# Second products' pools restacked, context steps spread, modulation stepped in the input projection

## Chip, cores, metric

The kernel runs on one core of a Trainium2 chip. The time is that of one launch on the device, in microseconds (us); runs are given by their median.

The engines are TensorE (PE, matrix products), VectorE (DVE), ScalarE (ACT) and GpSimd (POOL); SyncE (SP) issues most transfers between the chip's main memory and the on-chip memory. Each engine takes its instructions in order.

## What is computed

One trunk layer, for one group of 128 context tokens and one of 1024 latent tokens that share their weights, with D = 1024, 8 query and 2 key heads of 128, and an FFN of width 2816:

```python
def _swiglu(h, w1, w2):
    a, b = jnp.split(h @ w1, 2, axis=-1)
    return (jax.nn.silu(a) * b) @ w2
...
    sh1, sc1, g1, sh2, sc2, g2, sh3, sc3, g3 = [mod[:, i][:, None, :] for i in range(N_MOD)]
    f1 = _swiglu(_modulate(x, sh1, sc1), lw['ffn1_w1'], lw['ffn1_w2'])
    x = _layer_norm(ALPHA * x + 0.5 * g1 * f1, lw['ln_g'][0], lw['ln_b'][0])
    mix, k, v = _mixer(_modulate(x, sh2, sc2), lw, rope, kv_ctx)
    x = _layer_norm(ALPHA * x + g2 * mix, lw['ln_g'][1], lw['ln_b'][1])
    f2 = _swiglu(_modulate(x, sh3, sc3), lw['ffn2_w1'], lw['ffn2_w2'])
    x = _layer_norm(ALPHA * x + 0.5 * g3 * f2, lw['ln_g'][2], lw['ln_b'][2])
```

`_mixer` projects its input to queries, keys, values, pooling inputs (`pin`) and two gates, runs attention and a pooling branch side by side, and merges them. The modulation vectors are `silu(cond) @ w_mod + b_mod`, once for the context and once for the latents. All is float32.

## The kernel before

**Arithmetic.** Every float32 operand is split into a high and a low part: ACT writes the high part (L109), DVE subtracts it for the low one (L110). A product is then three matmuls (L132 to L134): high by high, high by low, low by high. `weight` loads a weight tile into one of five places `raw`, shared by all stages, and splits it into two `op` tiles. Splits of the second products' left operand are `so`, from a loaded tile `sr`.

**Stages**, in time: first FFN, up products (to 570 us) and second products (to 789); input projection of the mixer (to 1200); attention and pooling (to 1510); output side of the mixer (to 1761); second FFN, up products (to 2306) and second products (to the end). The projection works on three groups of 384 tokens (`project`, g = 0, 1, 2); attention begins while the last `pin` blocks are still to be done.

**The FFN.** Both products are formed by a scheme of seven products in place of eight (the up products A11, A12, S1, S2, S4, S3, A22; the second ones M1 to M7). `up` runs 18 pairs of column blocks (`up_pair`, m = 4 to 21). The second operand of A22 is the last to be read. In a pair, S3 and A22 add into the same PSUM bank Y; between them DVE has to read Y (`s5 += Y`, L572), and after A22 ACT takes its silu (L576).

**Work beside.** `tick` steps the generators in `side`: in the up stages the FFN of the context tokens (155 steps), in the projection the key and query tiles (norm, rotation, transposes on PE). When `side` is empty, a tick steps `mods` instead, the modulation of a later stage: a load of 512 KB of `w_mod` into a `raw` place and two DVE instructions with accumulation (L192, output `junk`), one to a step. `up_prod` ticks once or twice per product and steps `mods` once after A12, S2 and A22. In the projection `feature_block` (one weight tile, 24 matmuls of 384 columns) ticks once, `group_down` (the query weights, eight chunks of 18 matmuls) once per chunk. What is left of `mods` at the end of the projection is run in one go:

```python
                xT = nxt
            for _ in self.mods:
                pass
            self.flush()
```

**Memory.** At the end of the up stage its pools close, and `open_pools` opens the down stage's pools in the order of the list it is given, stacked from the lowest free address up. A tile of a down pool must wait until the up tiles that lay in its place have been read. In bytes per partition the stack before is, for the first FFN: `so` at 101920 to 126496, `op` to 151072, `sr` to 163360, then the rest. The first `so` lies over the place of the up stage's `op` tile that holds the weights of the last A22; places 126496 and up belonged to operands read earlier. For the second FFN it is: `op` at 92704 to 141856, `rest` to 162468, `so` to 211680, `sr` to 228064; the first `so` tiles lie over operands (`b2`) that the last A22 reads.

A scheduler then orders the instructions of each engine by a simulated time, so code order is not the order on an engine.

Of the kernel before, what the change touches and what calls it, by code (L numbers as in the profile page):

```python
# [32 lines left out]
P = 128  # L33
D = 1024
# [20 lines left out]
class Layer:  # L55
# [20 lines left out]
    def tick(self, n=1):  # L76
        for _ in range(n):
            while self.side:
                try:
                    next(self.side[0])  # L80
                    break
                except StopIteration:
                    self.side.popleft()
            else:
                next(self.mods, None)

    def flush(self):
        while self.side:
# [442 lines left out]
    def up_pair(self, m, w1, h_d):  # L531

        nc = self.nc
        add, sub = (partial(nc.vector.tensor_tensor, op=o) for o in (ALU.add, ALU.subtract))
        halves = lambda t: (t[:, :512], t[:, 512:])
        ra, rb = self.raw(w1[2 * m]), self.raw(w1[2 * m + 1])
        (b11, b21), (b12, b22) = halves(ra), halves(rb)
        hi, lo = self.wide(ra)
        Y = self.bank()
        self.up_prod(Y, "A11", (hi[:, :512], lo[:, :512]), True)  # L540
        s1 = self.tmp()
        nc.scalar.activation(s1, Y, AF.Copy)
        yield
        t = self.tsum()
        sub(t[:, 0, :], b12, b11)
        sub(t[:, 1, :], b22, t[:, 0, :])
        t12 = self.wide(self.flat(t))
        Z = self.bank()
        self.up_prod(Z, "A12", (hi[:, 512:], lo[:, 512:]), True, 2)
        add(s1, Z, s1)  # L550
        nc.scalar.activation(s1, s1, AF.Silu)
        yield
        w22 = self.wide(b22, 512)
        X = self.bank()
        self.up_prod(X, "S1", [halves(w)[0] for w in t12], True)
        s5 = self.tmp()
        nc.scalar.activation(s5, X, AF.Copy)
        yield
        sub(b11, t[:, 1, :], b11)
        sub(b21, b21, t[:, 1, :])  # L560
        t34 = self.wide(ra)
        self.up_prod(Y, "S2", [halves(w)[1] for w in t12], False, 2)
        u2 = self.tmp()
        nc.scalar.activation(u2, Y, AF.Copy)
        yield
        self.up_prod(X, "S4", w22, False)
        add(u2, X, u2)
        nc.vector.tensor_tensor(u2, u2, s1, ALU.mult)
        self.keep_h(m, 0, u2, h_d)
        yield  # L570
        self.up_prod(Y, "S3", [halves(w)[0] for w in t34], False)
        add(s5, Y, s5)  # L572
        yield
        self.up_prod(Y, "A22", [halves(w)[1] for w in t34], False)
        sa = self.tmp()
        nc.scalar.activation(sa, Y, AF.Silu)  # L576
        nc.vector.tensor_tensor(s5, s5, sa, ALU.mult)  # L577
        self.keep_h(m, 1, s5, h_d)
        self.h_sums(m, u2, s5, h_d)
        yield  # L580
# [200 lines left out]
        self.flush()  # L781

    def ctx_sum(self, i):
        y = self.t([P, 2, 512], "yc", bufs=1)
        with self.tc.issue_after(self.last_load):
            self.nc.sync.dma_start(self.flat(y), self.fc_d[i])
        return y

    def norms(self, i, res_of, dst):
# [8 lines left out]
        def residual(t):  # L798
            if last_stage(i):
                res = self.t([P, D], "tc", bufs=6, pool=self.pools["tc"])  # L800
            else:
                res = self.t([P, D], "res", bufs=2)
            with self.tc.issue_after(self.last_load):
                nc.sync.dma_start(res, res_of(t))
            return res

        def last(t, y):

            tt, stt = nc.vector.tensor_tensor, nc.vector.scalar_tensor_tensor
            res = residual(t)  # L810
            rs, mu, m2 = (self.t([P, 1], n) for n in ("rs", "mu", "mu2"))
            halves = [(y[:, h, :], slice(h * 512, (h + 1) * 512)) for h in range(2)]
            (y0, c0), (y1, c1) = halves
            for (v, cs), out in zip(halves, (None, m2)):
# [19 lines left out]
        def norm(t, y):  # L834
            y = self.flat(y)
            gate = gc if t == 0 else gl
            res = residual(t)
            rs = self.t([P, 1], "rs")
            mu = self.t([P, 1], "mu")
            nc.vector.tensor_tensor(y, y, gate, ALU.mult)  # L840
            yield
            nc.vector.scalar_tensor_tensor(y, res, ALPHA, y, ALU.mult, ALU.add, accum_out=mu)
# [13 lines left out]
    def ffn(self, i, head, res_of, dst, order, half, beside=None):  # L856
        a, tc = self.a, self.tc
        s = str(1 + i // 2)
# [15 lines left out]
        if beside:  # L874
            beside()
        with ExitStack() as st:
            self.open_pools(st, "down" + s, ("tc", "xr", "y", "so", "op", "sr", "rest") if i == 0 else ("tc", "y", "op", "rest", "so", "sr"))
            self.op_bufs = 6 if i == 0 else 12
            self.ph = self.pools["rest"]
            self.down(i // 2, a["w2_" + s], h_d, lambda: self.norms(i, res_of, dst), order, half, last_stage(i))  # L880
# [51 lines left out]
    def group_down(self, units, lhs):  # L932
        acc = [[self.bank() for _ in range(3)] for _ in range(2)]
        n = units.shape[0]
        for kc in range(n):
            w = self.weight(units[kc])
            self.tick()
            for j in range(3):
                self.down_unit(acc, w, lhs[kc], j, kc == 0, kc == n - 1)
        return acc  # L940
# [125 lines left out]
    def feature_block(self, w, xT):  # L1066
        wh, wl = self.weight(w)
        acc = self.bank()
        for kc in range(KC):
            if kc == 2:  # L1070
                self.tick()
            ks = slice(kc * P, (kc + 1) * P)
            x = xT[kc]
            self.mm3(acc[:, :GT], (wh[:, ks], wl[:, ks]), (x[:, 0, :], x[:, 1, :]), kc == 0, kc == KC - 1)
# [448 lines left out]
```

## Time and profile before

| | us |
|---|---|
| median of 3 runs | 2543.17 |
| range of the runs | 2539.73 to 2545.66 |
| profiled execution, its own time | 2543.56 |
| its span in the trace | 2541.8 |
| PE busy | 2459.1 |
| DVE busy | 1830.0 |
| ACT busy | 1213.7 |

The share of PE's busy time says how much standing still there is in all. The waits of PE say where it is and which instruction ended each wait; an instruction named `w` is a PSUM bank, `b` an up operand, `x` an input of the projection. The windows give the granted clock of TensorE in a stretch as a share of full speed: 1.00 is 2.4 GHz, 0.50 is 1.2 GHz, and a number between says how much of the stretch was at each. The timeline gives the start of each instruction, its duration, and in brackets the idle time before it and what ended it.

### The profile page before, as it was taken

What the parts mean: (1) busy time and instruction counts of PE and PEld (TensorE: products, weight loads), DVE (VectorE), ACT (ScalarE), POOL (GpSimd) and SP (SyncE); (2) the same over time, 40 slices, a digit from 0 to 9 for tenths busy, and PEclk for the clock granted to TensorE, in tenths of its full rate; (3) what the DMA queues carried; (4) which work ended last, traced back from release to release, by engine and by line L of the source; (5) the groups of instructions that cost most, each with busy time, mean ns of one, the idle gap of its engine ahead of it and who ended that gap; (6) DMA issues with size and microseconds to landing.
All of it is one profiled execution on the core that took longest, in us unless ns stands there. A gap on an engine that the chain in (4) does not pass through costs nothing.

```text
span 2541.8 us, 34077 instructions
## 1 busy us (share of the span) xinstructions
PE 2459.1 (97%) x12232; PEld 2121.8 (83%) x12232; DVE 1830.0 (72%) x2806; ACT 1213.7 (48%) x2092; POOL 462.4 (18%) x683
## 2 busy tenths in 40 slices
PE   8999999989999999999899999998899999998998
PEld 4888888868788989989899999997688888886886
DVE  6777778867678656468878876765777666766777
ACT  5544444434445344443777773433644444434442
POOL 0000011110023212132467640110000001011002
PEclk9999999999999999999999999999999999999999
DMA  7455567668675645545200024564455546568673
GB/s 290 137 180 184 183 233 246 225 228 290 215 257 209 221 173 176 177 142 187 79 2 1 1 97 159 205 213 151 137 192 179 178 165 229 195 220 305 233 249 124
DMA packets 163185, 461.63 MB, mean 182 GB/s; under 512 B 18756, under 2 KB 33396, under 8 KB 163016
## 3 DMA queue, kind: packets, MB, share of 16 engines
q1 hardware_dynamic: 140472, 377.60, 44.4%
q0 software_dynamic: 22400, 81.60, 8.6%
q8 instruction: 96, 1.57, 0.3%
q14 instruction: 73, 0.60, 0.1%
q10 hardware_dynamic: 144, 0.26, 0.0%
HBM read 388.32 MB, written 71.07 MB: 181 GB/s over the span
## 4 chain that ended last, share of the span: by engine, by line
PE 77%; issue 10%; DVE 5%; DMA 4%; ACT 2%; POOL 2%; SPq 0%; POOLq 0%; DVEq 0%; ACTq 0%
PE w L132 22%; PE w L134 22%; PE w L133 22%; PE w L928 8%; PE w L137 3%; DMA raw<-w 1%; DVE op L110 1%; DMA raw<-x 1%; DVE mx L1238 1%; DVE x L110 1%; DVE junk L192 1%; DMA raw<-w_mod 1%; PE w L226 0%; DMA sr<-h 0%; ACT pr L1246 0%
## 5 line engine op out<-in xcount | busy, mean ns | idle before, releaser
L110 DVE TENSOR_TENSOR op<-raw,op 128x1024 fp32r<-128x1024 f32 (+1 forms) x505 | 559.6, 1114 | 261.1 <-ACT op L109 222.9
L109 ACT ACTIVATE op<-raw 128x1024 fp32r<-128x1024 f32 (+1 forms) x505 | 483.5, 969 | 524.1 <-PE w L133 243.7
L132 PE MATMUL w<-b,op 128*128 128x512 f32 x880 | 344.8, 394 | 13.4 <-DVE tmp L572 8.5
L134 PE MATMUL w<-b,op 128*128 128x512 f32 x880 | 343.2, 392 | 2.2 <-DVE op L110 2.2
L133 PE MATMUL w<-b,op 128*128 128x512 f32 x880 | 345.0, 392 | 0.0
L132 PE MATMUL w<-x,op 128*128 128x384 f32 x768 | 262.4, 342 | 7.3 <-ACT op L109 6.3
L134 PE MATMUL w<-x,op 128*128 128x384 f32 x768 | 259.6, 340 | 3.4 <-DVE op L110 3.4
L133 PE MATMUL w<-x,op 128*128 128x384 f32 x768 | 260.3, 339 | 0.0
L132 PE MATMUL w<-op,so 128*128 128x512 f32 x616 | 237.9, 396 | 14.7 <-ACT op L109 11.1
L133 PE MATMUL w<-op,so 128*128 128x512 f32 x616 | 240.5, 390 | 1.0 <-DVE op L110 1.0
L134 PE MATMUL w<-op,so 128*128 128x512 f32 x616 | 240.1, 392 | 0.0
L132 PEld LDWEIGHTS w<-b,op 128*128 128x128 f32 x880 | 166.5, 189 | 50.6 <-DVE tmp L572 9.8
L513 POOL DMA_DIRECT2D h<-tmp x80 | 43.4, 543 | 879.2 <-DVE tmp L577 394.7
L134 PEld LDWEIGHTS w<-b,op 128*128 128x128 f32 x880 | 166.6, 189 | 37.5 <-DVE op L110 2.6
L133 PEld LDWEIGHTS w<-b,op 128*128 128x128 f32 x880 | 166.6, 189 | 34.1 <-DVE b L110 0.3
L1251 POOL TENSOR_TENSOR pr<-pr,sm 128x384 f32<-128x384 f32 x192 | 157.9, 851 | 92.2 <-DVE sm L1249 74.0
L109 ACT ACTIVATE so<-sr 128x1024 fp32r<-128x1024 f32 x84 | 82.3, 986 | 169.9 <-PE w L133 109.5
L132 PEld LDWEIGHTS w<-x,op 128*128 128x128 f32 x768 | 145.7, 190 | 8.9 <-ACT op L109 7.3
L192 DVE SCALAR_TENSOR_TENSOR junk<-raw,sil 128x1024 bf16<-128x1024 f32 x112 | 139.2, 1253 | 17.0 <-DMA raw<-w_mod 16.4
L132 PEld LDWEIGHTS w<-op,so 128*128 128x128 f32 x616 | 116.6, 190 | 39.9 <-ACT op L109 13.8
L134 PEld LDWEIGHTS w<-x,op 128*128 128x128 f32 x768 | 145.5, 190 | 3.8 <-DVE op L110 3.8
L133 PEld LDWEIGHTS w<-x,op 128*128 128x128 f32 x768 | 145.6, 190 | 0.3
(301 smaller groups left out, 5110.6 us busy)
## 6 DMA issues: line engine op xcount, KB each, us to landing
raw<-w SPq DMA_DIRECT2D x240, 256.0 KB, 5.3
raw<-w SPq DMA_DIRECT2D x116, 512.0 KB, 4.2
raw<-w1c SPq DMA_DIRECT2D x80, 512.0 KB, 3.4
sr<-h SPq DMA_DIRECT2D x70, 512.0 KB, 4.9
raw<-w_mod SPq DMA_DIRECT2D x56, 512.0 KB, 4.5
raw<-w_gate SPq DMA_DIRECT2D x48, 512.0 KB, 3.9
h<-tmp POOLq DMA_DIRECT2D x80, 256.0 KB, 3.9
h<-pc POOLq DMA_DIRECT2D x52, 256.0 KB, 4.3
```

Source lines behind the costliest of these rows:

```text
L109: self.nc.scalar.activation(hi, src, AF.Copy)
L110: self.nc.vector.tensor_tensor(lo, src, hi.bitcast(F32), ALU.subtract)
L132: mm(out, lhsT=lh, rhs=rh, start=start, stop=False)
L133: mm(out, lhsT=lh, rhs=rl, start=False, stop=False)
L134: mm(out, lhsT=ll, rhs=rh, start=False, stop=stop)
L137: self.nc.tensor.transpose(out, src, self.ident)
L192: nc.vector.scalar_tensor_tensor(junk, w, 1.0, self.sil[cond], ALU.mult, ALU.mult, accum_out=self.mod[:, cond, b : b + 1],)
L513: self.nc.gpsimd.dma_start(h_d[f // 2][:, 2 * kh + n, f % 2, :], h)
L928: self.nc.tensor.matmul(acc[h][j], lhsT=lhs[:, part, js], rhs=w[wi][:, h * 512 : (h + 1) * 512], start=f, stop=l)
L1238: nc.vector.tensor_reduce(mx[:, c : c + 1], b[:, :GT], AX.X, ALU.max)
L1251: nc.gpsimd.tensor_tensor(pr[:, c, :], pr[:, c, :], sm[:, 3:4].broadcast_to([P, GT]), ALU.mult)
```

## The change

Three edits. (1) `tick` no longer steps `mods` when `side` is empty; in the projection one step of `mods` is taken in each chunk of `group_down` and in each `feature_block`. (2) A12 of the up pairs ticks once instead of twice from m = 15 on, so that the 155 steps of the context FFN last until the last product. (3) The down stages' pools are stacked in another order, and the tiles `yc`, `res` have a pool of their own (`in`), in the second FFN `rs`, `mu`, `mu2` as well (`sm`).

```diff
@@ tick
-            else:
-                next(self.mods, None)
@@ up_pair
-        self.up_prod(Z, "A12", (hi[:, 512:], lo[:, 512:]), True, 2)
+        self.up_prod(Z, "A12", (hi[:, 512:], lo[:, 512:]), True, 2 if m < 15 else 1)
@@ ctx_sum, norms
-        y = self.t([P, 2, 512], "yc", bufs=1)
+        y = self.t([P, 2, 512], "yc", bufs=1, pool=self.pools["in"])
...
-                res = self.t([P, D], "res", bufs=2)
+                res = self.t([P, D], "res", bufs=2, pool=self.pools["in"])
...
+        def small(n):
+            return self.t([P, 1], n, pool=self.pools.get("sm"))
...
@@ the down stage
-            self.open_pools(st, "down" + s, ("tc", "xr", "y", "so", "op", "sr", "rest") if i == 0 else ("tc", "y", "op", "rest", "so", "sr"))
+            self.open_pools(st, "down" + s, ("tc", "xr", "y", "in", "so", "op", "sr", "rest") if i == 0 else ("tc", "y", "rest", "in", "sr", "op", "so", "sm"))
@@ group_down
             self.tick()
+            next(self.mods, None)
@@ feature_block
+            if kc == 5:
+                next(self.mods, None)
```

In bytes per partition the new stack is, for the first FFN: `in` 101920 to 114208, `so` to 138784, `op` to 163360, `sr` to 175648; `so` now lies over operands `b1`, which are last read in S1 and S2. For the second FFN: `rest` 92704 to 109088, `in` to 113184, `sr` to 129568, `op` to 178720, `so` to 227872. In the kernel after, line numbers differ by one or two: L110 is L108 there, L192 is L190, L572 is L570, L576 is L574, L1042 is L1044.

**First FFN, PE, the end of the up products.** `w_4404` is the bank Y of the last pair; `op_4521`, `op_4522` are the halves of A22's weights, `b_...` its operand; `w_4625` and on are M1's banks. Before:

```order
L133 MATMUL w_4404<-b_140_765,op_4521 128x512
L134 MATMUL w_4404<-b_140_765,op_4522 128x512
L132 MATMUL w_4404<-b_145_794,op_4521 128x512
L133 MATMUL w_4404<-b_145_794,op_4521 128x512
L134 MATMUL w_4404<-b_145_794,op_4522 128x512
L132 MATMUL w_4625<-op_4650,so_4643 128x512
L133 MATMUL w_4625<-op_4651,so_4643 128x512
L132 MATMUL w_4626<-op_4650,so_4643 128x512
L133 MATMUL w_4626<-op_4651,so_4643 128x512
L132 MATMUL w_4627<-op_4650,so_4643 128x512
```

After (bank Y is `w_4371`), where the last pair's S3 ends:

```order
L130 MATMUL w_4371<-b_144_791,op_4500 128x512
L131 MATMUL w_4371<-b_144_791,op_4500 128x512
L132 MATMUL w_4371<-b_144_791,op_4501 128x512
L130 MATMUL w_4628<-op_4653,so_4646 128x512
L130 MATMUL w_4629<-op_4653,so_4646 128x512
L130 MATMUL w_4630<-op_4653,so_4646 128x512
L130 MATMUL w_4631<-op_4653,so_4646 128x512
L131 MATMUL w_4628<-op_4654,so_4646 128x512
```

and where its A22 stands:

```order
L132 MATMUL w_4629<-op_4690,so_4684 128x512
L130 MATMUL w_4629<-op_4690,so_4683 128x512
L131 MATMUL w_4629<-op_4691,so_4683 128x512
L132 MATMUL w_4629<-op_4690,so_4684 128x512
L130 MATMUL w_4371<-b_130_707,op_4500 128x512
L131 MATMUL w_4371<-b_130_707,op_4500 128x512
L132 MATMUL w_4371<-b_130_707,op_4501 128x512
```

M1 stood behind the last A22; now M1 begins right after S3, and 36 of its matmuls precede A22.

**First FFN, ACT, same place.** Before:

```order
L557 ACTIVATE tmp_4517<-w_4504 128x512
L564 ACTIVATE tmp_4537<-w_4404 128x512
L109 ACTIVATE op_4650<-raw_4647 128x1024
L109 ACTIVATE op_4687<-raw_4684 128x1024
L109 ACTIVATE op_4724<-raw_4721 128x1024
L576 ACTIVATE tmp_4579<-w_4404 128x512
L109 ACTIVATE so_4643<-sr_4641 128x1024
L109 ACTIVATE so_4680<-sr_4678 128x1024
```

After:

```order
L562 ACTIVATE tmp_4528<-w_4371 128x512
L107 ACTIVATE so_4646<-sr_4644 128x1024
L107 ACTIVATE op_4653<-raw_4650 128x1024
L107 ACTIVATE so_4683<-sr_4681 128x1024
L107 ACTIVATE op_4690<-raw_4687 128x1024
L107 ACTIVATE so_4720<-sr_4718 128x1024
L107 ACTIVATE op_4727<-raw_4724 128x1024
L492 ACTIVATE pc_4560<-w_1499 128x512
L492 ACTIVATE pc_4576<-w_1500 128x512
L107 ACTIVATE so_4757<-sr_4755 128x1024
L107 ACTIVATE op_4764<-raw_4761 128x1024
L574 ACTIVATE tmp_4579<-w_4371 128x512
```

The first `so` stood behind the silu of A22 (L576); now three `so` and three `op` stand ahead of it (L574).

**Second FFN, ACT, the end of the up products.** Before:

```order
L564 ACTIVATE tmp_21129<-w_20998 128x512
L576 ACTIVATE tmp_21171<-w_20998 128x512
L109 ACTIVATE so_21229<-sr_21227 128x1024
L109 ACTIVATE so_21266<-sr_21264 128x1024
L109 ACTIVATE so_21303<-sr_21301 128x1024
L109 ACTIVATE so_21340<-sr_21338 128x1024
L109 ACTIVATE so_21377<-sr_21375 128x1024
L109 ACTIVATE so_21390<-sr_21388 128x512
L109 ACTIVATE op_21236<-raw_21233 128x1024
L109 ACTIVATE op_21273<-raw_21270 128x1024
```

After:

```order
L492 ACTIVATE pc_21172<-w_18196 128x512
L574 ACTIVATE tmp_21175<-w_20969 128x512
L107 ACTIVATE so_21239<-sr_21237 128x1024
L107 ACTIVATE op_21246<-raw_21243 128x1024
L107 ACTIVATE so_21276<-sr_21274 128x1024
L107 ACTIVATE op_21283<-raw_21280 128x1024
L107 ACTIVATE so_21313<-sr_21311 128x1024
```

On both sides the silu of the last A22 comes first; behind it six `so` ran before the first `op`, and now they alternate. On PE the last A22 precedes M1 on both sides.

**Input projection, DVE, from the last query weights of the first group to the second group's first blocks.** `ss` is the reduction of a query tile, `qn` its scaled form, `qr` its rotated one, `rt` a help tile of the rotation. Before:

```order
L1042 TENSOR_REDUCE ss_7693<-qn_7690 128x8
L110 TENSOR_TENSOR op_7772<-raw_7769,op_7771 128x1024
L1046 TENSOR_TENSOR qn_7699<-w_7399,rr_7695 128x512
L1046 TENSOR_TENSOR qn_7699<-w_7402,rr_7695 128x512
L997 TENSOR_TENSOR qr_7702<-qn_7699,tb_7705 128x8x64
L998 TENSOR_TENSOR rt_7710<-qn_7699,tb_7705 128x512
L997 TENSOR_TENSOR qr_7702<-qn_7699,tb_7705 128x8x64
L110 TENSOR_TENSOR op_7811<-raw_7808,op_7810 128x1024
L999 TENSOR_TENSOR qr_7702<-qr_7702,rt_7710 128x8x64
L998 TENSOR_TENSOR rt_7714<-qn_7699,tb_7705 128x512
L110 TENSOR_TENSOR op_7851<-raw_7848,op_7850 128x1024
L999 TENSOR_TENSOR qr_7702<-qr_7702,rt_7714 128x8x64
```

After, from the same reduction on:

```order
L1044 TENSOR_REDUCE ss_7727<-qn_7724 128x8
L190 SCALAR_TENSOR_TENSOR junk_7797,mod<-raw_7795,sil_70 128x1024
L108 TENSOR_TENSOR op_7776<-raw_7773,op_7775 128x1024
L190 SCALAR_TENSOR_TENSOR junk_7838,mod<-raw_7795,sil_71 128x1024
L108 TENSOR_TENSOR op_7812<-raw_7809,op_7811 128x1024
L1048 TENSOR_TENSOR qn_7733<-w_7409,rr_7729 128x512
L1048 TENSOR_TENSOR qn_7733<-w_7412,rr_7729 128x512
L190 SCALAR_TENSOR_TENSOR junk_7881,mod<-raw_7879,sil_70 128x1024
L108 TENSOR_TENSOR op_7853<-raw_7850,op_7852 128x1024
L999 TENSOR_TENSOR qr_7736<-qn_7733,tb_7739 128x8x64
L1000 TENSOR_TENSOR rt_7744<-qn_7733,tb_7739 128x512
L999 TENSOR_TENSOR qr_7736<-qn_7733,tb_7739 128x8x64
```

and on to the last addition of that `qr`:

```order
L190 SCALAR_TENSOR_TENSOR junk_7944,mod<-raw_7879,sil_71 128x1024
L200 TENSOR_TENSOR md_85<-mod,bmod 128x8
L108 TENSOR_TENSOR op_7897<-raw_7894,op_7896 128x1024
L1001 TENSOR_TENSOR qr_7736<-qr_7736,rt_7744 128x8x64
L200 TENSOR_TENSOR md_85<-mod,bmod 128x8
L190 SCALAR_TENSOR_TENSOR junk_8030,mod<-raw_8028,sil_70 128x1024
L108 TENSOR_TENSOR op_7959<-raw_7956,op_7958 128x1024
L1000 TENSOR_TENSOR rt_7748<-qn_7733,tb_7739 128x512
L190 SCALAR_TENSOR_TENSOR junk_8092,mod<-raw_8028,sil_71 128x1024
L1001 TENSOR_TENSOR qr_7736<-qr_7736,rt_7748 128x8x64
```

Between the reduction and the last addition there stood three splits; now there stand five splits, six modulation steps and two small ones (L200). On PE the transposes of this tile stand behind the same three blocks, 72 matmuls, on both sides. The loads of `w_mod` that stood as a run of eleven at the end of the projection on SP now stand singly among its weight loads.

## Rows read from the trace of the kernel before

**Rows 1.** The page: span; busy us, share and instructions of engines.

```profile
span 2541.8 us, 34077 instructions
...
PE 2459.1 (97%) x12232; PEld 2121.8 (83%) x12232; DVE 1830.0 (72%) x2806; ACT 1213.7 (48%) x2092; POOL 462.4 (18%) x683
```

**Rows 2.** Waits of PE at 525–575: us in total, times, longest us.

```profile
PE w L132 <- DVE tmp L572: 7.7, 2, 4.1
PE w L132 <- ACT so L109: 1.7, 1, 1.7
```

**Rows 3.** Windows: length, busy of five engines, granted clock, DMA share, GB/s.

```profile
530.00:540.00 10.00, 5.95 (x19) 4.46 (x19) 8.04 (x13) 1.33 (x2) 2.90 (x5) 0.78 0.65 225
540.00:550.00 10.00, 10.00 (x41) 8.11 (x41) 5.09 (x8) 4.29 (x7) 1.26 (x2) 0.88 0.40 125
560.00:570.00 10.00, 6.18 (x19) 4.09 (x18) 3.65 (x4) 1.18 (x3) 0.54 (x1) 0.83 0.77 274
940.00:950.00 10.00, 10.00 (x62) 9.93 (x62) 8.64 (x11) 5.05 (x10) 4.71 (x7) 1.00 0.37 121
1210.00:1220.00 10.00, 8.77 (x37) 8.46 (x38) 9.96 (x17) 5.20 (x10) 2.59 (x2) 0.76 0.73 226
1230.00:1240.00 10.00, 5.47 (x27) 4.96 (x27) 8.25 (x22) 5.66 (x17) 3.59 (x4) 0.83 0.15 52
```

**Rows 4.** Waits of PE at 1195–1245, start of attention.

```profile
PE w L134 <- DVE op L110: 3.4, 1, 3.4
PE w L132 <- ACT op L109: 2.4, 1, 2.4
PE w L137 <- DVE mx L1242: 2.3, 1, 2.3
PE w L137 <- DVE dl L110: 2.2, 1, 2.2
PE w L132 <- ACT pin L1087: 0.9, 1, 0.9
```

**Rows 5.** Group of DVE at 1185–1240: count, busy us, mean ns, idle.

```profile
L192 DVE SCALAR_TENSOR_TENSOR junk<-raw,sil 128x1024 bf16<-128x1024 f32 x18 | 25.4, 1413 | 0.3
```

**Rows 6.** Timeline of PE, second FFN's boundary: start, us, instruction, wait.

```profile
2305.81 0.39 PE L133 MATMUL w<-b,op 128*128 128x512 f32 x1
2306.04 0.39 PE L134 MATMUL w<-b,op 128*128 128x512 f32 x1
2317.53 2.07 PE L132 MATMUL w<-op,so 128*128 128x512 f32 x4 [11.10 <-ACT op L109]
2319.40 0.63 PE L133 MATMUL w<-op,so 128*128 128x512 f32 x1
```

**Rows 7.** Timeline of ACT in the same stretch.

```profile
2306.96 3.88 ACT L109 ACTIVATE so<-sr 128x1024 fp32r<-128x1024 f32 x4
2313.29 1.06 ACT L109 ACTIVATE so<-sr 128x1024 fp32r<-128x1024 f32 x1 [2.45 <-DMA sr<-h]
```

**Rows 8.** Timeline of DVE in the same stretch.

```profile
2308.43 1.22 DVE L110 TENSOR_TENSOR so<-sr,so 128x1024 fp32r<-128x1024 f32 x1
```

**Rows 9.** Timeline of DVE, turn from first to second group.

```profile
932.80 1.22 DVE L1042 TENSOR_REDUCE ss<-qn 128x8 f32<-128x1024 f32 x1 [0.91 <-ACT qn L1040]
...
937.49 1.29 DVE L1046 TENSOR_TENSOR qn<-w,rr 128x512 f32<-128x512 f32 x2 [1.89 <-POOL rr L988]
...
944.22 0.82 DVE L999 TENSOR_TENSOR qr<-qr,rt 128x512 f32<-128x512 f32 x1
```

**Rows 10.** Timeline of PE there, the first transposes of a query tile.

```profile
946.12 0.60 PE L137 MATMUL w<-ident,qr 128*128 128x128 f32 x4
```

**Rows 11.** Source line L192 (ns min/median/max), then timelines of DVE and POOL.

```profile
L192 DVE SCALAR_TENSOR_TENSOR junk<-raw,sil x112: 1206/1219/4218, 126.5 to 1991.9; 128x1024 bf16<-128x1024 f32 x112
...
1201.95 4.22 DVE L192 SCALAR_TENSOR_TENSOR junk<-raw,sil 128x1024 bf16<-128x1024 f32 x1
...
1201.23 3.85 POOL L1159 TENSOR_TENSOR pl<-pin 128x296 f32<-128x296 f32 x6
```

More of the change, by code (lines that the diff above doesn't have):

```diff
@@ L810, in last @@
             res = residual(t)
-            rs, mu, m2 = (self.t([P, 1], n) for n in ("rs", "mu", "mu2"))
+            rs, mu, m2 = (small(n) for n in ("rs", "mu", "mu2"))
             halves = [(y[:, h, :], slice(h * 512, (h + 1) * 512)) for h in range(2)]
@@ L837, in norm @@
             res = residual(t)
-            rs = self.t([P, 1], "rs")
-            mu = self.t([P, 1], "mu")
+            rs = small("rs")
+            mu = small("mu")
             nc.vector.tensor_tensor(y, y, gate, ALU.mult)
```

## Prediction

> **What bounds the kernel now.** I read the busy shares first: TensorE (PE) runs in 97% of the span [rows 1], so time is won only where PE stands still or runs at the lower of its two clocks. The whole idle time is 2541.8 − 2459.1 = 82.7 us, and no change of order can win more than this and the clock that idle stretches cost. So I listed the waits of PE, and read the three stretches that the change touches, with the granted clock beside them.
>
> End of the first FFN's up products: PE waits twice for the DVE addition L572 (7.7 us) and once for the split of the first stacked operand (1.7) [rows 2]. The clock is 0.78 and 0.88 in 530–550 and 0.83 in 560–570 [rows 3]: 4.4, 2.4 and 3.4 us at 1.2 GHz, 10.2 in all. In the first slice PE is busy for 5.95 us and waits for the rest; I count one microsecond of the low clock into that wait, so PE ran some 9.2 us at half speed, which lost 4.6. Sum 9.4 + 4.6 = 14.0.
>
> Start of attention: five waits, 3.4 + 2.4 + 2.3 + 2.2 + 0.9 = 11.2 us [rows 4]. Of the clock, 1210–1220 has 0.76 and 1230–1240 has 0.83 [rows 3], 4.8 and 3.4 us at 1.2 GHz, nearly all of it running: 4.1 lost. Sum 15.3. DVE is what is late here: eighteen modulation steps (L192, `junk`) take 25.4 of its 55 us [rows 5]; the loop at the end of the input projection drains them in one heap.
>
> End of the second FFN's up products: the last A22 matmul starts at 2306.04, the first M1 matmul at 2317.53, after 11.1 us [rows 6]. ScalarE (ACT) shows why: after L576 it splits all the `so`, six of them, and comes to the first `op` only after them [rows 7]; the fifth and sixth `so` wait for their loads, the fifth 2.45 us. The first four matmuls then take 1.87 us to the fifth [rows 6], about half speed, and if this lasts 3.4 us, as in the slice 560–570 [rows 3], 1.7 are lost. Sum 12.8.
>
> **The change part by part.**
>
> *First FFN.* The stacked operands no longer lie over the place that A22's weights hold until the last product, and the slowed ticks leave context steps for the last pair. The order after the change shows it: on PE 36 matmuls of M1 stand between the last pair's S3 and its A22, which waits for L572 (L570 after), and 24 of other products do so in the pair before; ahead of the wait on ACT three `so` and three `op` are split. A matmul of this size follows the last one after 0.23 us [rows 6], so 24 cover 5.5 us and 36 cover 8.3, against the longest wait of 4.1 [rows 2]. The 1.7 us for the first `so` goes too, since it is split before A22. What is late next is the load of these `so`, issued while the DMA engines are 0.77 busy [rows 3]. I take 12.5 of the 14.0 as won and leave one small wait of about 1.5, the size of the smallest there; bounds 6 (one of the two large waits stays, with its clock) and 14.
>
> *Second FFN.* Here the order of PE is unchanged: A22 ends, then M1. ACT still takes L576 first, but then one `so`, one `op`, and so on. Worked out with the rows: `so` starts at 2306.96 and four take 3.88, so 0.97 each [rows 7]; one `so` and one `op` are ready at 2306.96 + 1.94 = 2308.9, and PE starts there, 2.5 us after A22's end at 2306.43. Its four matmuls with the high parts take 0.9 us at full and 1.87 at half clock [rows 6]. Then it needs the low part of `op`: DVE reaches the low part of `so` at 2308.43 for 1.22 [rows 8], then comes one addition of half a tile, 0.6, as the scalings in [rows 9], then `op` for 1.2, so 2311.4. That is 0.6 to 1.5 us more of waiting: 3.1 to 4.0 in place of 11.1, a gain of 7.1 to 8.0. The clock afterwards may cost from nothing to 3.4 us, against 1.7 now. I take 7; bounds 3 (the `so` loads arrive no earlier, and the second `so` waits as the fifth does now) and 9.5.
>
> *Start of attention.* Modulation is finished in the projection of the second group, so the 22 drained steps with their eleven 512 KB loads leave this stretch, and the loads of pooling and of the late blocks move up in SP's queue. DVE's 55 us lose the 25.4 [rows 5], so it is half idle. All five waits are behind DVE or the shared load places; I take 13 of 15.3 and leave one wait of 2.3, the one for the maximum L1242 [rows 4], which depends on the scores and not only on the heap. Bounds 8 and 15.3.
>
> *Where the steps go.* The same 22 steps, 1.27 us each from start to start with their accumulator read, 28 us in all, now lie in the projection, one half-chunk per block. Where DVE has room they cost nothing. It has none at the turn from the first to the second group. There the query tile `qr` has to pass DVE before PE transposes it. Before: reduction at 932.80, one split, the scaling at 937.49 (after 1.89 us idle, waiting for POOL's power), rotation with two more splits, the last addition at 944.22 for 0.82 [rows 9]; PE takes the transposes at 946.12 [rows 10], so the slack is 1.1 us. After, between the same reduction and the same last addition stand six modulation steps and five splits instead of none and three. Chain: 932.8 + reduction 1.2 + six steps 6 × 1.15 + five splits 5 × 1.14 + two scalings 1.2 + six rotation steps 6 × 0.61 = 932.8 + 18.7 = 951.5. PE has the same 72 matmuls of three blocks in front of the transposes, so it stands from 946.1 to 951.5: 5.4 us, and behind a stall that long the trace shows a half clock for 3.4 us or more (after the one of 4.1 it ran 5.8 us so), 1.7 to 2.9 lost. I take 8. Lower bound 0: the window 940–950 has DVE busy for 8.64 of 10 with PE full [rows 3], so a neighbouring load of this kind is carried today. Upper bound 14: a second stall of the same size at the next query tile, without the clock. The first group's keys have steps beside them before as after. The second group's keys and the five load places, which the extra loads now share with the query weights, get 1 us; bounds 0 and 5.
>
> *Elsewhere.* Mixer output, the second FFN's head and the rest of both down stages keep their order on SP; the small tiles `rs`, `mu` only change address. Nought.
>
> **Sum** on the profiled execution, 2543.56 us (its span is 2541.8, and it lies 0.4 above the median of 2543.17, so no correction): 2543.6 − 12.5 − 7 − 13 + 8 + 1 = 2520.1, taken as 2520.
>
> **A rule against the change.** The longest modulation step took 4218 ns where the median is 1219, and it ran while POOL was in its own additions L1159, which began 0.7 us before it and ended 1.0 us before its end [rows 11]. The Trainium skill, "SBUF — State Buffer", section "SBUF: two separate sides", says that VectorE and GpSimd share a port pair held for a whole instruction, also by a VectorE operation with two SBUF inputs against a GpSimd operation that reads SBUF; a modulation step is such an operation, and the row agrees, but for one of 112 only. What the row means here as a mechanism is the last rival.
>
> **The rivals.**
> (a) *DVE's lookahead absorbs the steps.* No stall at the turn of the groups and none at the keys: 2520 − 9 = 2511. For it: DVE idles 1.89 us for POOL in that chain [rows 9], some steps fall into it, and a block or two of split weights lies ready ahead of PE. Against: the six steps stand behind the reduction, and PE cannot pass its transposes.
> (b) *The end of the first FFN gives its gain back.* M1 is put ahead of A22, so a late `so` load now blocks A22 as well. For it: `so` waits for its load in the second FFN. If one wait of 4.1 with its clock (2.9) and 3 us of further waits in M1 stay, 2520 + 10 = 2530. The same time comes out if the second FFN gains nothing and 3 us are lost beside it.
> (c) *The modulation steps cost their full length.* All 22 on PE's path: 28 us in place of 9, 2520 + 19 = 2539, within 0.2% of before. It needs DVE late in all of the second group's start, not at one place.
> (d) *Slower: DVE and POOL block one another.* In the projection POOL does each tile's powers and rotation tables. If a moved step that meets them takes 4.2 instead of 1.2 us, each costs 3.0, and DVE is on the path there. Slower by more than 5 us from (32.5 − 9 + 5) / 3.0 = 9.5 such steps, ten of the 22; twelve give 2556. Against: of the 112 steps in the whole kernel, among them those beside the first group's keys, one has that length.
>
> **How the numbers follow.** A measurement of this kernel tells about 0.2%, 5 us, from no change. Forecast 2520 with 0.50; (a) 2511 with 0.20; (b) 2530 with 0.17; (c) 0.08; (d) 0.05. The sum of all upper gains without the new stalls is 14 + 9.5 + 15.3 = 38.8, 2505; the lower gains (6 + 3 + 8) with both stalls (14 + 5) are a loss of 2 against before. The range of 8 in 10 takes in (a), the forecast and (b), with their bounds of a few us: 2506 to 2537. Faster: 0.50 + 0.20 + 0.17 = 0.87; same: (c), 0.08; slower: (d), 0.05.
>
> **What would show it.** In the profile after: no wait for L572 above 1 us at 525–575, and M1's matmuls ahead of the last A22; at the second FFN's boundary an idle time of PE of 3 to 4 us instead of 11.1, ended by `op`; no L192 after the projection, and at most one wait over 2 us at the start of attention; a new PE wait for `qr`'s splits or rotation, some 5 us, about 12 us after the last query matmul of the first group, with a clock below 0.9 in that slice. The prediction is wrong if this last wait is missing (then 2511) or is one of several, or if PE waits for `so` loads in M1.

## The result

| | before | after |
|---|---|---|
| median, us | 2542.37 (4 runs) | 2518.35 (4 runs) |
| range, us | 2539.73 to 2545.66 | 2515.13 to 2519.96 |
| profiled execution / its span | 2543.56 / 2541.8 | 2515.13 / 2513.3 |

The ratio is 0.9903, 95% interval 0.9886 to 0.9920. The forecast was 2520. The profiled execution is the fastest of the four, 3.2 us under the median, so a difference of the two profiles shows some 4 us more than the medians do.

The following table is worked out from the two traces: a stage runs from one marked matmul to the next; *idle* is the time in which no matmul ran, *clock* is half of the time in which PE ran at 1.2 GHz, which is what that clock cost.

| stretch | before: us (idle, clock) | after: us (idle, clock) | difference | forecast |
|---|---|---|---|---|
| from 520 us to the projection's first matmul | 269.0 (12.6, 6.3) | 249.1 (0.1, 0.0) | −19.9 | −12.5 |
| to the first score matmul (projection) | 410.7 (4.3, 3.0) | 425.0 (14.9, 6.2) | +14.3 | +9 |
| to the last score matmul (attention) | 296.6 (16.2, 4.0) | 285.0 (6.7, 3.4) | −11.5 | −13 |
| from there to the second FFN's last A22 | 807.6 | 803.9 | −3.6 | 0 |
| from the last A22 to the last matmul | 227.0 (11.1, 1.6) | 219.1 (3.8, 2.9) | −7.9 | −7 |

The span and the busy line of PE after [rows 1]:

```profile
span 2513.3 us, 34071 instructions
...
PE 2451.0 (98%) x12232; PEld 2120.7 (84%) x12232; DVE 1827.2 (73%) x2806; ACT 1213.7 (48%) x2092; POOL 460.9 (18%) x683
```

**End of the first FFN.** At 520–720 the list of PE's waits is empty after the change; before it held 12.6 us, 9.4 of them the two lines of [rows 2]. The timeline of PE (start, length, instruction) shows the passage: M1 begins on the beat of the up products, 0.23 us after the last S3 matmul.

```profile
553.57 0.39 PE L132 MATMUL w<-b,op 128*128 128x512 f32 x1
553.80 1.07 PE L130 MATMUL w<-op,so 128*128 128x512 f32 x4
554.70 0.39 PE L131 MATMUL w<-op,so 128*128 128x512 f32 x1
```

**Projection.** The waits of PE at 765–1260 (us in all, times, longest) have four waits for the rotated tiles `qr`; before had one there, of 0.2 us:

```profile
PE w L135 <- DVE qr L1001: 10.6, 4, 5.9
PE w L135 <- ACT pr L1250: 2.0, 1, 2.0
```

The longest is the one that was forecast. On DVE (timeline, rows left out) the chain runs from the reduction to the last addition, with the six modulation steps L190 in it; PE's transposes L135 start 0.15 us after that addition's end, where [rows 9, 10] had them right behind the blocks:

```profile
917.94 1.21 DVE L1044 TENSOR_REDUCE ss<-qn 128x8 f32<-128x1024 f32 x1
919.07 1.22 DVE L190 SCALAR_TENSOR_TENSOR junk<-raw,sil 128x1024 bf16<-128x1024 f32 x1
...
935.07 1.22 DVE L190 SCALAR_TENSOR_TENSOR junk<-raw,sil 128x1024 bf16<-128x1024 f32 x1
...
936.21 0.80 DVE L1001 TENSOR_TENSOR qr<-qr,rt 128x512 f32<-128x512 f32 x1
```

```profile
930.90 0.33 PE L132 MATMUL w<-x,op 128*128 128x384 f32 x1
937.16 1.09 PE L135 MATMUL w<-ident,qr 128*128 128x128 f32 x4 [5.93 <-DVE qr L1001]
```

917.94 to 937.01 are 19.1 us; the working gave 18.7. The windows (columns as in [rows 3]) show DVE nearly full before the wait and the clock around it:

```profile
850.00:860.00 10.00, 6.48 (x30) 6.16 (x29) 8.99 (x22) 2.72 (x5) 4.63 (x8) 0.83 0.68 212
920.00:930.00 10.00, 10.00 (x59) 10.00 (x58) 9.87 (x15) 3.55 (x5) 3.64 (x3) 1.00 0.76 251
930.00:940.00 10.00, 4.07 (x19) 3.69 (x18) 9.37 (x16) 3.18 (x6) 4.20 (x6) 0.72 0.73 218
```

The first of these rows holds the second wait, 3.5 us at the first group's keys, which the forecast did not have.

**Start of attention.** Of the five waits of [rows 4] none is left at 1180–1245; one of 2.0 us, for an exponential (L1250, above), stands in their place. No L190 stands among DVE's groups at 1185–1240 [rows 5].

**End of the second FFN.** The waits of PE at 2275–2300, and the timeline behind the last A22 matmul [rows 6]:

```profile
PE w L130 <- ACT op L107: 2.6, 1, 2.6
PE w L131 <- DVE op L108: 1.2, 1, 1.2
PE w L130 <- DVE tmp L570: 0.8, 1, 0.8
```

```profile
2285.24 0.39 PE L132 MATMUL w<-b,op 128*128 128x512 f32 x1
2288.20 1.19 PE L130 MATMUL w<-op,so 128*128 128x512 f32 x4 [2.58 <-ACT op L107]
2290.64 0.80 PE L131 MATMUL w<-op,so 128*128 128x512 f32 x1 [1.24 <-DVE op L108]
2291.23 0.63 PE L132 MATMUL w<-op,so 128*128 128x512 f32 x1
```

2.58 and 1.24 were worked out as 2.5 and 0.6 to 1.5. The four matmuls in between still ran at the full clock; those after 2290.6 follow one another at 0.43 us, half of it.

### The profile page after: what moved, and what is told of

Same layout as the page of the kernel before. It is cut to its first block, busy times and chain, and to the rows that moved or that the text cites. A ratio compares the mean times of both kernels' runs of the same rounds, so it can differ in the third digit from the quotient of the medians.

```text
span 2513.3 us, 34071 instructions
## 1 busy us (share of the span) xinstructions
PE 2451.0 (98%) x12232; PEld 2120.7 (84%) x12232; DVE 1827.2 (73%) x2806; ACT 1213.7 (48%) x2092; POOL 460.9 (18%) x683
## 4 chain that ended last, share of the span: by engine, by line
PE 82%; DVE 6%; issue 5%; DMA 3%; ACT 2%; POOL 1%; SPq 0%; POOLq 0%; DVEq 0%; ACTq 0%
PE w L130 24%; PE w L132 24%; PE w L131 24%; PE w L929 8%; PE w L135 3%; DVE op L108 1%; DMA raw<-w_mod 1%; DMA raw<-w 1%; DVE x L108 1%; DVE mx L1242 1%; ACT pr L1250 1%; DVE junk L190 1%; PE w L224 0%; DMA raw<-x 0%; DMA raw<-w1c 0%
## 5 line engine op out<-in xcount | busy, mean ns | idle before, releaser
L108 DVE TENSOR_TENSOR op<-raw,op 128x1024 fp32r<-128x1024 f32 (+1 forms) x505 | 560.4, 1116 | 271.2 <-ACT op L107 214.8
L190 DVE SCALAR_TENSOR_TENSOR junk<-raw,sil 128x1024 bf16<-128x1024 f32 x112 | 135.8, 1224 | 27.1 <-DMA raw<-w_mod 26.5
L131 PE MATMUL w<-ax,op 128*128 128x512 f32 x352 | 139.4, 396 | 1.4 <-DVE ax L108 1.4
```

The lines of the kernel that those rows point to most:

```text
L108: self.nc.vector.tensor_tensor(lo, src, hi.bitcast(F32), ALU.subtract)
L131: mm(out, lhsT=lh, rhs=rl, start=False, stop=False)
L190: nc.vector.scalar_tensor_tensor(junk, w, 1.0, self.sil[cond], ALU.mult, ALU.mult, accum_out=self.mod[:, cond, b : b + 1],)
```

## Experiments

Theory: each part acts at its own place, and the moved steps cost where they stand in a tile's chain on DVE. The rivals are in the expectations. The columns of this table are the stretches of the one above, in us, from each kernel's trace; the ratio is that of its runs to the runs of before beside it, with its interval.

| kernel | ratio | to the projection | projection | attention | from last A22 |
|---|---|---|---|---|---|
| before | 1 | 269.0 | 410.7 | 296.6 | 227.0 |
| e1_stack1 | 0.9970 (0.9960–0.9980) | 259.6 | 413.6 | 298.2 | 227.1 |
| e2_ticks | 0.9974 (0.9962–0.9987) | 254.9 | 410.4 | 295.6 | 230.6 |
| e3_stack2 | 0.9964 (0.9951–0.9977) | 264.9 | 411.5 | 298.7 | 218.8 |
| e4_mods | 1.0005 (0.9991–1.0020) | 267.5 | 425.9 | 283.8 | 227.3 |
| e5_after | 0.9916 (0.9899–0.9933) | 251.0 | 425.2 | 283.9 | 219.3 |
| e6_no_mods | 0.9893 (0.9875–0.9911) | 248.4 | 411.5 | 295.1 | 218.2 |
| e7_noturn | 0.9923 (0.9906–0.9940) | 250.2 | 434.5 | 285.6 | 218.5 |
| e8_quiet | 0.9888 (0.9871–0.9904) | 251.2 | 421.2 | 282.9 | 218.1 |
| e9_two | 0.9894 (0.9878–0.9911) | 251.2 | 422.2 | 284.2 | 217.8 |
| e10_g1 | 0.9849 (0.9833–0.9865) | 250.4 | 416.1 | 282.7 | 219.2 |

One order of instructions gives different stretches in different profiles. The changed kernel and e5_after differ by up to 1.9 us. Before and e3_stack2 have the same order on PE, DVE, ACT and POOL up to 2307 us, and yet 269.0 and 264.9 us in the first stretch; e4_mods, the same up to 842 us, has 267.5. So some 4 us of a difference in that column can be chance.

**e1_stack1: the first FFN's pools alone.**

(Here and in e3_stack2 the tiles named in the change lie in `in` and `sm` where the stack has these pools.)

```diff
-("tc", "xr", "y", "so", "op", "sr", "rest") if i == 0
+("tc", "xr", "y", "in", "so", "op", "sr", "rest") if i == 0
```

> Only the first FFN's second-product pools are restacked; ticks, modulation and the second FFN as before. Theory (each part acts at its own place): 33 matmuls of M1 then stand between the last pair's S3 and A22, so of the first FFN's boundary the second wait for L572 (3.7 us), its low clock (1.7) and the wait for the first so (1.7) go, 7 us; the wait of 4.05 in the pair before, with 2.9 of low clock, stays. With the two small waits in the down stage (1.0 and 1.9 with 1.7 of low clock), if they too come from the place of the pools, 11.5. So 7 to 11.5 us faster than before. Rival (stack and ticks need each other): under 3 us. Rival (stack alone does all): 18 to 19 us, as the changed kernel shows from 520 us to the start of the projection.

2533.84 us beside 2540.24 of before. The waits of PE at 520–720 keep one for L572, the one of the pair before the last; the second and that for `so` are gone:

```profile
PE w L132 <- DVE tmp L572: 3.9, 1, 3.9
PE w L132 <- DVE y L752: 1.3, 1, 1.3
```

The stretch is 9.4 us shorter than before's (5.3 than e3_stack2's), the runs 0.3% (7.6 us): the theory's size.

**e2_ticks: A12's ticks alone.**

```diff
-        self.up_prod(Z, "A12", (hi[:, 512:], lo[:, 512:]), True, 2)
+        self.up_prod(Z, "A12", (hi[:, 512:], lo[:, 512:]), True, 2 if m < 15 else 1)
```

> Only A12 ticks once from pair 15 on; pools and modulation as before. Theory (own place): context steps then cover the wait for L572 in the pair before the last (4.05 us and 2.9 of low clock), the last pair keeps its wait of 3.7 and the wait for the first so, since M1 still stands behind A22: 7 us faster. Rival (needs the restack): within 2 us of before. Rival (ticks alone do all): 14 us or more.

2532.51 us, 6.6 us by the ratio. The same list:

```profile
PE w L132 <- ACT so L109: 1.6, 1, 1.6
PE w L132 <- DVE y L752: 1.4, 1, 1.4
PE w L132 <- DVE tmp L572: 1.2, 1, 1.2
```

The long wait of the pair before the last is gone, as expected, and of the last pair's 3.7 us 1.2 is left, which was not: the context steps cover most of it too. So the two parts overlap in the last pair: against before's 269.0 the stretch gains 9.4 and 14.1 alone and 18 to 20 together. The runs gain less than the stretch of e2_ticks, in part because the second FFN's boundary, with its old stack, got longer there, 13.5 us of waiting for 11.1 (waits at 2280–2320):

```profile
PE w L132 <- ACT op L109: 13.5, 1, 13.5
```

**e3_stack2: the second FFN's pools alone.**

```diff
-else ("tc", "y", "op", "rest", "so", "sr")
+else ("tc", "y", "rest", "in", "sr", "op", "so", "sm")
```

> Only the second FFN's second-product pools are restacked. Theory: the wait of 11.1 us at its boundary becomes two, some 2.6 and 1.2, and the time from the last A22 to the end falls by the 7.9 us that the changed kernel shows; the rest of the trace keeps its stages. 6 to 8 us faster than before. Rival (the gain is bought by the earlier arrival of this stage in the changed kernel): less than 3 us.

2530.91 us; the last stretch is 8.2 us shorter. Its waits at 2295–2320 are nearly those of the changed kernel:

```profile
PE w L132 <- ACT op L109: 2.6, 1, 2.6
PE w L133 <- DVE op L110: 0.9, 1, 0.9
PE w L132 <- DVE tmp L572: 0.8, 1, 0.8
```

**e4_mods: the modulation steps alone.**

```diff
-            else:
-                next(self.mods, None)
@@ group_down
             self.tick()
+            next(self.mods, None)
@@ feature_block
+            if kc == 5:
+                next(self.mods, None)
```

> Only the modulation steps are moved (none in ticks, one per chunk and block of the projection); pools and A12's ticks as before. Theory: the projection becomes some 14 us longer (two waits for rotated tiles, 3.5 and 5.9, with their low clock), the stretch of attention after it 11.5 us shorter, net 2 to 4 us slower than before or no difference that the runs can tell. Rival (my forecast's size, 13 won and 9 lost): 4 us faster. Rival (these waits come from the two FFN parts shifting the projection against its loads): no new waits, 11 us faster.

2543.23 us beside 2540.24, no difference that the runs can tell. The projection is 15.2 us longer, attention 12.8 shorter, and the waits for rotated tiles are there without the other parts (at 765–1260):

```profile
PE w L135 <- DVE qr L1001: 10.5, 5, 6.0
```

So these waits belong to the steps' places, not to a shift against the loads. The product of the four ratios, 0.9970 × 0.9974 × 0.9964 × 1.0005 = 0.9913, is that of the whole change (0.9903 and 0.9916): within what the runs tell, the parts add up. The four intervals leave some 6 us either way, so the overlap of two parts seen above fits as well.

**e5_after and e6_no_mods: the changed kernel again, and the same without its modulation part.**

> The changed kernel again, beside the next three on the same chip. By all theories 22 to 26 us faster than before (0.990 to 0.9915); two waits for rotated tiles, about 3.5 us at the first group's keys and 5.9 us at the second group's first query tile.

> The changed kernel without its modulation part: pools and ticks as changed, modulation as before (drained at the end of the projection). Theory (the modulation part wins 11.5 us at attention and loses 14 in the projection): as fast as the changed kernel or up to 3 us faster, 24 to 27 us below before. Rival (my forecast, 13 won for 9 lost): 4 us slower than the changed kernel, 20 below before.

2517.23 and 2511.46 us. Without the moved steps the projection has the length of before (411.5) and attention too (295.1). The changed kernel's modulation part loses 13.7 us in the projection and wins 11.2 behind it, 2.5 lost by the stretches and 6 by the ratios, whose intervals overlap. My forecast's +9 and −13 would have put e6_no_mods 4 us above the changed kernel, at a ratio of 0.993; that lies outside its interval.

**e7_noturn: no steps at the turn of the groups.**

```diff
@@ group_down
-            next(self.mods, None)
+            if kc < 6:
+                next(self.mods, None)
@@ feature_block
-            if kc == 5:
+            if kc == 5 and steps:
@@ pin blocks
-            acc = self.feature_block(a["w_pin"][i], xT)
+            acc = self.feature_block(a["w_pin"][i], xT, g == 0)
```

(`steps` is true for all other blocks.)

> The changed kernel, but no modulation step in the last two chunks of the query weights and in the pin blocks of the second and third group. In DVE's order two steps instead of six then stand between the first query tile's reduction and its last addition, and four splits instead of five. Theory (the chain on DVE sets the wait, about 1.15 us a step and 1.14 a split): the chain is 4 x 1.15 + 1.14 = 5.7 us shorter, so the wait of 5.9 us shrinks to under 1 us and its low clock of some 3 us goes too; the wait at the first group's keys (3.5) stays. 8 to 9 us faster than the changed kernel. Rival (the wait comes from POOL's powers or from the loads of w_mod in the shared places): the wait stays above 3 us.

2519.98 us: no faster than the changed kernel. The projection is 9 us longer in its profile, which lies 3.5 us above the median of its runs. The first query tile's wait is gone, as the chain says (13.3 us in place of 19.1), but others have grown. The waits of PE at 925–960 and at 765–1260:

```profile
PE w L135 <- DVE qr L1002: 5.0, 1, 5.0
```

```profile
PE w L135 <- DVE qr L1002: 14.0, 4, 5.0
```

The wait at 948 is the second query tile's; its chain, from the reduction at 937.90 to the last addition's end at 953.3, is 15.4 us long, against 9.8 in the changed kernel. Three steps stand in it instead of two, three splits instead of none, and DVE waited 2.15 us for POOL's powers. So it is mostly splits that moved from the first tile's chain into the second's, and one step. A third wait, 3.3 us in the third group, has no step in its chain at all, but three splits and 2.8 us for POOL's powers. The expectation counted one tile and not what comes up at the next ones.

**e8_quiet: steps where no key or query work is pending, two in each of six query chunks.**

```diff
@@ group_down
-            next(self.mods, None)
+            if kc < 6:
+                next(self.mods, None)
+                next(self.mods, None)
@@ feature_block
-            if kc == 5:
+            if kc == 5 and not self.side:
```

> The changed kernel with the modulation steps where DVE has room: two in each of the first six chunks of the query weights, one in a block only when no key or query steps are pending. No step stands in the first query tile's chain, and the second group's keys have fewer. Theory: both waits for rotated tiles go with their low clock, 14 us, and the start of attention keeps what it won, so some 12 to 14 us faster than the changed kernel, 36 to 38 below before. Rival (DVE and the five load places are then short in the query chunks themselves, with two steps and a 512 KB load more per chunk): new waits there of 5 us or more, under 6 us faster than the changed kernel.

2511.21 us, 7 us faster than the changed kernel by the ratios, whose intervals just overlap: half of what the theory said. The waits for `qr` at 765–1260 fall from 10.6 to 3.6 us; the one left is in the third group, in whose query chunks the last steps fell beside the second group's query tiles. A new one of 2.3 us lies in the query chunks, at the transposes of a tile loaded there (L135, released by a split on ACT):

```profile
PE w L135 <- DVE qr L1003: 3.6, 1, 3.6
PE w L135 <- ACT op L107: 2.3, 1, 2.3
```

**e9_two: two steps in each free block, one in seven query chunks.**

```diff
@@ group_down
-            next(self.mods, None)
+            if kc < 7:
+                next(self.mods, None)
@@ feature_block
-            if kc == 5:
-                next(self.mods, None)
+            if kc == 5 and not self.side:
+                next(self.mods, None)
+                next(self.mods, None)
```

> The changed kernel with the modulation steps placed by what the last runs showed: two in a block that has no key or query steps pending (most of them in the first twelve blocks of the first group), one in each of the first seven chunks of the query weights, none elsewhere. In DVE's order no step then stands between the first query tile's reduction and the last tile's last addition, in the second group and in the third; four stand beside the first group's keys. Theory (the order on DVE inside each tile's chain sets the waits): the projection is back at the 411 us that it takes without the moved steps, attention keeps its 284, so about 14 us faster than the changed kernel, 2503, and 35 to 38 below before (0.985 to 0.9865). Rival (DVE and the five load places as a whole are too short for the steps in the projection, so that a wait comes up wherever they lie): waits of 5 us or more at the first blocks or in the query chunks, no faster than 2511.

2514.46 us. The waits for `qr` fall to 0.2 us. In the second group the first two query tiles' chains are free of steps; in the third tile's stand four, which was not expected, but it ends at 965.57 and PE comes to its transposes only at 966.38. At the start of the projection, though, a wait of 6.7 has come up (waits of PE at 780–830):

```profile
PE w L130 <- ACT op L107: 9.9, 3, 6.7
```

SP's queue shows what PE waits for, the second gate weights. The first are issued at 784.43; the place that comes free at 791.3, after a split on DVE, goes to a load of `w_mod`, and behind it stand the small loads of the stage:

```profile
784.43 0.33 SPq L111 DMA_DIRECT2D raw<-w_gate  x1
791.30 0.33 SPq L111 DMA_DIRECT2D raw<-w_mod  x1
...
794.25 1.27 SPq L979 DMA_DIRECT2D cs<-rope  x2
795.56 0.67 SPq L111 DMA_DIRECT2D raw<-w_gate  x1
```

The second gate weights are issued at 795.56. The last small load was out at 795.51, and a modulation step on DVE, which can free a place `raw`, had ended at 795.4; the trace does not say which of the two it was that counted. e10_g1 changes the order.

**e10_g1: as e9_two, one step in each of the first group's pin blocks.**

```diff
@@ group_down, on top of e9_two
             if kc < 7:
                 next(self.mods, None)
+                if kc < 2:
+                    next(self.mods, None)
@@ feature_block, on top of e9_two
             if kc == 5 and not self.side:
-                next(self.mods, None)
-                next(self.mods, None)
+                for _ in range(steps):
+                    next(self.mods, None)
```

(`steps` is 1 in the pin blocks and 2 in the gate blocks.)

> As the last kernel (e9_two), but the four pin blocks at the start of the projection take one modulation step each as in the changed kernel, and the first two chunks of the query weights two. Theory (the wait of 6.7 us at the start came from a w_mod load in each of the first blocks, ahead of the first gate weights in the five places; the tiles' chains are free of steps): the wait at the start falls back to the two of some 2 us that the kernel before has there too, no wait for rotated tiles above 1 us, projection 410 to 414 us, 2503 to 2506 in all, 0.985 to 0.987 of before. Rival (a wait of this size comes up elsewhere in the projection): no faster than 2511, 0.989.

2504.59 us, ratio 0.9849: 0.67% below the changed kernel's 0.9916, clear of both intervals. The largest waits of PE at 780–1245:

```profile
PE w L135 <- DMA raw<-x: 2.7, 2, 1.5
PE w L130 <- ACT op L107: 2.2, 2, 1.5
PE w L135 <- ACT pr L1254: 2.0, 1, 2.0
PE w L253 <- DVE gt L249: 1.9, 1, 1.9
```

On SP the second gate weights now take the place that comes free at 791.6, ahead of the small loads, and the wait at the start is 1.5:

```profile
784.75 0.33 SPq L111 DMA_DIRECT2D raw<-w_mod  x1
791.62 0.33 SPq L111 DMA_DIRECT2D raw<-w_gate  x1
```

The projection takes 416.1, within some 5 us of what it takes without the moved steps, and attention keeps its 282.7. This is the version that beats both kernels: the change's own idea, with the steps kept out of the chains that PE waits for (the third tile's has four again, and PE comes 1 us after it) and a gate load ahead of `w_mod`'s at the start. It is also 0.44% (11 us) below e6_no_mods, which leaves the steps in their heap, clear of both intervals.

## Why the prediction was right, point by point

**First FFN, −12.5 forecast.** The mechanism stood: 36 matmuls of M1 ahead of A22, and no wait left. The term was too small, −18 to −20 in two profiles against before's, −14 to −16 against e3_stack2's stretch of the same order. I left one wait of 1.5 us standing, and none stayed. And I counted only the boundary; the down stage before had two waits of 1.9 and 1.0 us and some low clock, together 4 to 5, that are small or gone after (waits of PE before, at 520–720):

```profile
PE w L132 <- DVE y L752: 1.9, 1, 1.9
PE w L133 <- DVE op L110: 1.0, 1, 1.0
```

In e3_stack2, at the same window and in the same order, they are

```profile
PE w L132 <- DVE y L752: 0.7, 1, 0.7
PE w L133 <- DVE op L110: 0.5, 1, 0.5
```

so part of their shrinking is no effect of the change. The one for L752 has 1.3 and 1.4 us in e1 and e2, and in the kernels with both parts lies between nothing and 1.5. Split by part, the restack took the last pair's wait and the ticks that of the pair before, as worked out, and the ticks most of the last pair's as well.

**Second FFN, −7 forecast.** −7.9 and −7.7. The two waits came out within 0.1 us and inside the range given. Rival (b)'s second half (no gain there) fell.

**Start of attention, −13 forecast.** −11.5 and −12.7. I left one wait of 2.3 us; one of 2.0 is there, though of an exponential and not of the maximum L1242, so its size is luck. What I did not leave is the low clock in this stretch, which cost 1.7 to 3.4 us.

**Projection, +9 forecast.** +14.3 and +14.5: the one term that was mis-sized to the bad side. The turn of the groups was right (wait 5.93 for 5.4, chain 19.1 for 18.7). The step that failed is the sentence that the first group's keys have steps beside them before as after. Before, a tick with key work pending steps no modulation; after, one step falls in every block, so two stand inside the first key tile's chain, and PE waits 3.5 us there with 1.7 of low clock. Their own length, 2 × 1.15 us, is the smaller part: in front of the first, DVE stood idle for 3.28 us, waiting for that step's load of `w_mod`, and the reduction behind it had to wait too:

```profile
843.43 0.41 DVE L1012 TENSOR_TENSOR qn<-kvs 128x256 f32<-128x256 f32 x1
847.12 1.23 DVE L190 SCALAR_TENSOR_TENSOR junk<-raw,sil 128x1024 bf16<-128x1024 f32 x1 [3.28 <-DMA raw<-w_mod]
848.27 0.42 DVE L1014 TENSOR_REDUCE ss<-qn 128x2 f32<-128x256 f32 x1
...
854.62 0.44 PE L135 MATMUL w<-ident,qr 128*128 128x128 f32 x2 [3.52 <-DVE qr L1001]
```

The same idle time stands there in e4_mods (3.1), e5_after (3.6) and e7_noturn (4.0). Before, this chain ended at 870.4 and PE came to it at 871.9. By that slack the two steps alone would have made PE wait for about 0.8 us, an estimate that no run tests; the forecast had a price for a step in a chain, but none there for the step's load. With waits of 0.9 and 0.2 at later tiles this makes up the difference. The prediction had also said that it would be wrong if the wait at the turn were one of several: by that sign of its own it was wrong here, for PE waits four times for `qr`. Rival (a), no stall, fell with e4_mods; rival (c), the steps' full 28 us on PE's path, did not come either.

**Rival (d), DVE and POOL.** The row of the longest step after reads 1369 ns, against 4218 before [rows 11]:

```profile
L190 DVE SCALAR_TENSOR_TENSOR junk<-raw,sil x112: 1214/1220/1369, 126.0 to 1971.1; 128x1024 bf16<-128x1024 f32 x112
```

With 22 steps moved among POOL's powers and rotation tables none was held for long, so the rival fell, and the 3.0 us that the one long step took too much are gone. The long step belongs to the heap: its 4217 to 4227 ns stand in each of the five kernels that drain the heap, and no step is longer than 1420 in the others. The Trainium skill, "SBUF — State Buffer", section "SBUF: two separate sides", lets such a step and a POOL operation that reads SBUF exclude each other for a whole instruction. The one row of before fits a hold of this kind, though over several POOL instructions in a row and not one (the last of them ended 1.1 us before the step did, not 1.0). The moved steps do not show it: in the changed kernel one ran its usual 1.22 us inside a POOL operation of 2.53 (POOL's spans in the trace are rough):

```profile
920.43 2.53 POOL L988 TENSOR_TENSOR rr<-rr,mhalf 128x8 f32<-128x8 f32 x1
921.35 1.22 DVE L190 SCALAR_TENSOR_TENSOR junk<-raw,sil 128x1024 bf16<-128x1024 f32 x1
```

**Sum.** −12.5 − 7 − 13 + 9 = −23.5 against −24.0 in the medians. The total is closer than its terms, and that is luck: between 1 and 7 us too little at the first FFN, by the profile that one compares with, and the 3.6 us won where nought was forecast stand against 5 too little in the projection; and the five stretches of the two profiles add up to −28.6, which is 4.6 more than the medians gained.

## What to carry to other kernels

When work is moved off a late engine's heap into earlier blocks, count it in each dependent chain that it will stand in, one chain per tile, and follow the scheduler's order over all of them: what is taken out of one chain lets other work into the next. Count a step's load too, for on an engine that works in order a step that waits for its load holds what stands behind it. At the start of a stage the load that the busy engine needs first has to stand ahead of the background loads. Before stacking pools, ask which tile of the old stage is read last and put under it what the new stage needs last.

## What was not expected

The four matmuls between the two waits at the second FFN's boundary ran at the full clock, and the granted clock fell to half only with the second, shorter wait; the low clock there cost 2.9 us after a wait of 2.6 and 1.2, against 1.6 after one of 11.1. That is no fixed price: with the same two waits it cost 1.7 us in e8_quiet, 1.5 in e9_two and 3.0 in e10_g1. And spreading steps evenly over free blocks (e9_two) cost more at one place, 6.7 us, than the key and query chains it set free had cost singly.
